# Own latents of the samples over all 128 rows, and new start addresses for the tiles that TensorE reads

## Chip, cores, metric

One NeuronCore of a Trainium2 chip runs the whole program in one launch. The metric is device time in microseconds (us) of that core, as the median of several runs. The profile is one further execution with the hardware profiler on. Engines are named as in the profile: PE (TensorE matmuls), PEld (TensorE weight loads), DVE (VectorE), ACT (ScalarE), POOL (GpSimd), SP (the queue that issues nearly all transfers).

## The reference, cut to what matters

Two layers (`DEPTH = 2`) of a streaming encoder for 256 prompt frames and 8 samples of 16 frames, 384 rows in all, width 1024:

```python
x += 0.5 * post_norm(SwiGLU(pre_norm(x)))      # FFN 1, D_FF = 2816
n  = pre_norm(x); h = n @ w_in                 # MLA, conv, gMLP, short conv, 4 gates
y  = sum_b sigmoid(gate_b) * (branch_b @ w_br_b);  x += post_norm(y @ w_o)
x += 0.5 * post_norm(SwiGLU(pre_norm(x)))      # FFN 2
# MLA of a sample: its 16 frames read 256 cached latents and their own 16
prob = softmax(mla_scores(q_nope, q_rope, concat([cache_lat, latent]), ...))
```

For a sample the kernel keeps everything in the latent space: the probabilities of its 128 rows (8 heads by 16 frames) over 256 cached and 16 own latents are multiplied by those 272 latents of 256 numbers.

## The kernel before

**Matmuls.** Each fp32 weight block is loaded into a staging tile `st` (4 buffers), rounded by ACT into `wh`, and DVE writes the rest, `st - wh`, as `wl`. Activations are split the same way (`xh`, `xl`; `hh`, `hl`; `mh`, `ml`; `bh*`, `bl*`). `mm3` (line 304) issues three fp32r matmuls for each product: high by high, low by high, high by low. `wh` and `wl` live in two rings: ring M (36 KB for each partition, mixer) and ring F (50 KB, feed-forward).

**Order.** The program hands every engine its instructions in an order written out by hand: a small planner (`tick`, `spawn`, `need`) counts estimated times and lets the follow-up work of ACT, DVE and POOL fall between PE's matmuls. PE's own order is a fixed stream with fillers.

**Stages of one layer.** `ffn_head` and `ffn_body` (line 489): for each of 20 chunks of hidden channels after the first two, two gate-up halves of 8 x 3 matmuls that stream 384 columns of `xh` or `xl` past a weight block (called "p" below), and 18 that stream 512 columns of a down weight past `hh` or `hl` ("d"). Heads (line 367) keep `xh` as the stationary operand and stream the weights. `mixer_front` (line 636) has the projections, the prompt's attention and the samples' attention, with `dense()` as the source of fillers; `mixer_merge` the gates (8 x 3 matmuls of 384 columns against a block of ring M) and the branch products; `mixer_out` the product with `w_o` (`mh`, `ml` stationary, 512 columns of ring M streaming).

**A sample's attention** (lines 1099 to 1137). `load_ct` loads the sample's cached latents `ct` and copies its 16 own rows of `lat_s` to partitions 0 to 15 of `nl` with a DMA. `sample` does the softmax over 272 columns. `sample_out` transposes the probabilities in three pieces, 128, 128 and 16 columns, copies them out (ACT two pieces into `ps[:, 0:2]`, DVE the 16 rows into `ps[0:S, 2]`), and multiplies: for each half k of the latents two fp32 matmuls over 128 rows (`ct`) and one over 16 rows (`nl`). In the trace each fp32 matmul stands as two.

**Addresses.** A tile occupies the same range in every partition, and pools stand one behind the other from byte 16512, each tile rounded up to 32 bytes. Adding up the sizes in the order of allocation gives where tiles start; a slice of 128 or 512 columns moves the start by a multiple of 512 bytes, so the place within 512 bytes is that of the tile:

| tiles | start, bytes past a multiple of 512, before | the same after, from the numbers in the diff |
|---|---|---|
| `xh`, `xl`, `ident`, `ones` | 192 | 0 |
| staging `st` | 448 | 192 |
| ring M `wh`, `wl` | 448 (8 `wl` at 192) | 0 (those 8 at 256) |
| `half` | 448 | 0 |
| ring F `wh`, `wl`; `hh`, `hl`; `bh*`, `bl*`; `aT`, `yT*` | 256 | 0 |
| `mh`, `ml` | 480 | 0 |
| `cqh`, `cql`, `lth`, `ltl`, `kT`, `qTp`, `qa` | 160 | a multiple of 64 |
| `qTs`, `lat_s`, `ct`, `pTs` | 32 | a multiple of 64 |

Of the kernel before, what the change touches and what calls it, by code (L numbers as in the profile page):

```python
# [8 lines left out]
F32 = mybir.dt.float32  # L9
F32R = mybir.dt.float32r  # L10
BF16 = mybir.dt.bfloat16
AF = mybir.ActivationFunctionType
ALU = mybir.AluOpType
AX = mybir.AxisListType
PSUM = bass.MemoryType.PSUM

P = 128
D = 1024
KD = D // P
T = 384  # L20
NT = 3
# [5 lines left out]
S = 16  # L27
NP = TP // S
PAST = 256
H = 8  # L30
ND = 64
RD = 32
QL = 384
KL = 256
CW = 31
SM_SCALE = (ND + RD) ** -0.5
NEG = -1e30
TAIL = 4
LAG = 2
RING_M = 36  # L40
RING_F = 50
STAGE = 4
# [4 lines left out]
PE, ACT, DVE, POOL = "tensor", "scalar", "vector", "gpsimd"  # L47
# [50 lines left out]
class Core:  # L98
    def __init__(self, tc, a, depth):
        self.tc, self.a, self.depth = tc, a, depth  # L100
        self.nc = Chip(self)


    def plan_units(self):

# [216 lines left out]
        return self.nt.tile([P, 512], F32, tag="half", name="half", bufs=4)  # L322

    def junk(self, n):
        return self.nt.tile([P, 512], BF16, tag="junk", name="junk", bufs=2)[:, :n]

    def bank(self):
        self.bk = (self.bk + 1) % 6
# [257 lines left out]
    def mixer_consts(self, l):  # L586
        nc, a = self.nc, self.a
        q = self.mc
        m = {}
        for name, shape in (("rows", [1152]), ("cols", [74]), ("gbias", [2, P]), ("wst", [4, P])):  # L590
            m[name] = q.tile([P] + shape, F32, tag=name, name=name)
        nc.sync.dma_start(out=m["rows"], in_=a["rows"][l].partition_broadcast(P))
        nc.sync.dma_start(out=m["cols"], in_=a["cols"][l])
        nc.sync.dma_start(out=m["gbias"], in_=a["gbias"][l])
        nc.sync.dma_start(out=m["wst"], in_=a["wst"][l])
        bd = m["bd"] = q.tile([P, 4, P], F32, tag="bd", name="bd")
        nc.gpsimd.memset(bd, 0.0)
        for b in range(NB):
            nc.sync.dma_start(out=bd[b * S:(b + 1) * S, :, b * S:(b + 1) * S], in_=a["wst"][l, 0:S, :, 0:S])
        nc.gpsimd.memset(m["wst"][64:128, :, 0:64], 0.0)  # L600
        return m
# [15 lines left out]
    def mixer(self, l, m):  # L617

        nc, tc, a = self.nc, self.tc, self.a
        pool = lambda name, bufs=1: tc.tile_pool(name=name, bufs=bufs, reuse_waits="tile")  # L620
        self.mo_ctx = tc.tile_pool(name="mixo", bufs=1, side="right", reuse_waits="tile")
        with pool("mixp") as mp:
            aT = mp.tile([P, 4, T], F32, name="aT")
            self.th = {(0, g): mp.tile([P, T], F32, name=f"th{g}") for g in range(3)}
            yT = {b: mp.tile([P, 2, T], F32, name="yT" + b) for b in "bcd"}
            with pool("mixf") as mf, pool("mixa") as ma:
                self.mixer_front(l, m, mf, ma, aT, yT)
            mo = self.mo_ctx.__enter__()
            mh = mo.tile([P, KD, T], F32R, name="mh")
            ml = mo.tile([P, KD, T], F32R, name="ml")  # L630
            with pool("mixm") as mm_:
                self.mixer_merge(l, mm_, aT, yT, mh, ml)
        self.open_ring()
        return self.mixer_out(l, mh, ml, self.load_gain(a["mix_norm_post"][l]))

    def mixer_front(self, l, m, mf, ma, aT, yT):
        nc, tc, a = self.nc, self.tc, self.a
        mm = nc.tensor.matmul
        rows, cols = m["rows"], m["cols"]
# [2 lines left out]
                                 cols[:, 66:68], cols[:, 68:74].rearrange("p (m k) -> p m k", m=2))  # L642
        pool = lambda name, bufs=1: tc.tile_pool(name=name, bufs=bufs, reuse_waits="tile")
        vn = [mf.tile([P, 256], F32, name=f"vn{t}") for t in range(NT)]
        qTs = ma.tile([P, 4, P], F32, name="qTs")
        qr0 = ma.tile([96, NB, H * S], F32, name="qr0")
        qrs = ma.tile([P, 2, H * S], F32, name="qrs")
        krT = ma.tile([96, T], F32, name="krT")
        lat_s = ma.tile([P, KL], F32, name="lat_s")
# [187 lines left out]
        with pool("mixq") as mq:  # L837
# [122 lines left out]
            for hp in range(4):  # L960
                w = self.weights(("uq", l, hp))
                for i in range(2):
                    h = 2 * hp + i
                    o = self.bank()[:, :T]
# [22 lines left out]
            for j in range(4):  # L987
                o = self.bank()[:, :TP]
# [5 lines left out]
            for t in range(2):  # L994
                o = self.bank()
# [78 lines left out]
        with pool("mixs") as ms:  # L1074
# [22 lines left out]
            cts = {}  # L1097

            def load_ct(b):
                ct = ms.tile([P, 2, KL], F32, tag="ct", name="ct", bufs=4)  # L1100
                nc.sync.dma_start(out=ct, in_=a["cache"][l, b].rearrange("(k p) c -> p k c", p=P))
                nl = ms.tile([S, KL], F32, tag="nl", name="nl", bufs=4)
                nc.sync.dma_start(out=nl, in_=lat_s[b * S:(b + 1) * S, :])
                cts[b] = ct, nl

            for b in range(2, 5):
                load_cT(b, ms)

            def sample(b, sb):
                ct, nl = cts.pop(b)  # L1110
                yield PE
                p = self.half()[:, :PAST + S].unsqueeze(1)
                yield from self.softmax(p, sb.unsqueeze(1), 1)
                self.drop("acc")
                self.spawn(("att",), sample_out(b, p, ct, nl))

            def sample_out(b, p, ct, nl):
                yield DVE
                pt = self.acc(2, 0)
                for k in range(2):  # L1120
                    nc.tensor.transpose(pt[:, k * P:(k + 1) * P], p[:, 0, k * P:(k + 1) * P], self.ident)
                nc.tensor.transpose(pt[0:S, 256:384], p[:, 0, PAST:], self.ident)
                self.drop("half")
                yield PE
                ps = ms.tile([P, 3, P], F32, tag="pTs", name="pTs", bufs=2)
                nc.scalar.copy(ps[:, 0:2, :], pt[:, 0:256].rearrange("p (a b) -> p a b", a=2))
                nc.vector.tensor_copy(ps[0:S, 2, :], pt[0:S, 256:384])
                self.drop("acc")
                yield ACT
                o = self.acc(2, 1)[:, :256].rearrange("p (a b) -> p a b", a=2)  # L1130
                for k in range(2):
                    ksl = slice(k * P, (k + 1) * P)
                    for kc in range(2):
                        mm(o[:, k, :], lhsT=ct[:, kc, ksl], rhs=ps[:, kc, :], start=(kc == 0), stop=False)
                    mm(o[:, k, :], lhsT=nl[:, ksl], rhs=ps[0:S, 2, :], start=False, stop=True)
                yield PE
                nc.scalar.copy(qa[:, :, b, :], o)

# [128 lines left out]
    def run(self):  # L1267
        nc, tc, a = self.nc, self.tc, self.a
        self.units = self.plan_units()
        self.index = {u[0]: i for i, u in enumerate(self.units)}  # L1270
        self.next_unit = self.at = 0
        self.staged, self.live, self.arrival = [], {}, 0.0
        self.spans, self.ring_at, self.size = {"M": {}, "F": {}}, {"M": 0, "F": 0}, {"M": RING_M * 1024, "F": RING_F * 1024}
        self.now, self.seq, self.busy, self.queue, self.idle = 0.0, 0, False, [], []
# [4 lines left out]
        with ExitStack() as es:  # L1279
            pool = lambda name, bufs=1, **kw: es.enter_context(tc.tile_pool(name=name, bufs=bufs, **kw))  # L1280
            const = pool("const")
            self.stage = pool("stage", STAGE)
            self.rings = {"M": pool("ringm").ring(RING_M * 1024), "F": None}
            self.nt = pool("nt")
            self.gains = pool("gains", 2)
# [4 lines left out]
            self.dummy = const.tile([P, 1], F32, name="dummy")  # L1290
            self.neghalf = const.tile([P, 1], F32, name="neghalf")
            nc.vector.memset(self.neghalf, -0.5)
            self.ones = const.tile([P, P], F32, name="ones")
            nc.vector.memset(self.ones, 1.0 / 256)
            self.x = [const.tile([P, D], F32, name=f"x{t}") for t in range(NT)]
# [5 lines left out]
            self.load_unit()  # L1301
            self.ident = const.tile([P, P], F32, name="ident")
            nc.scalar.dma_start(out=self.ident, in_=a["ident"])
            self.xh = const.tile([P, KD, T], F32R, name="xh")
            self.xl = const.tile([P, KD, T], F32R, name="xl")

# [18 lines left out]
            for l in range(self.depth):  # L1325
                m = {}

                def consts():
                    if l == 0:
                        self.rope_t = const.tile([P, NT, 2 * RD], F32, name="rope_t")  # L1330
                        nc.sync.dma_start(out=self.rope_t, in_=a["rope_t"])
                        self.rope_f = const.tile([P, T], F32, name="rope_f")
                        nc.sync.dma_start(out=self.rope_f, in_=a["rope_f"])
                    m.update(self.mixer_consts(l))

                self.ffn_head("ffn1", l)
                tail, post = self.ffn_body("ffn1", l, hook=consts)
                nc.scalar.activation(self.dummy, self.neghalf, AF.Exp)
                self.tails(tail, post, self.load_gain(a["mix_norm_pre"][l]))
                self.close_ffn_pool()  # L1340
                self.close_ring()
                tail, post = self.mixer(l, m)
                self.tails(tail, post, self.load_gain(a["ffn2_norm_pre"][l]))
                self.mo_ctx.__exit__(None, None, None)
                self.ffn_pool()
                self.ffn_head("ffn2", l)
                last = l + 1 == self.depth
                tail, post = self.ffn_body("ffn2", l, a["o_y"] if last else None)
                self.tails(tail, post, None if last else self.load_gain(a["ffn1_norm_pre"][l + 1]))
# [135 lines left out]
```

## Time and profile before

| | |
|---|---|
| three runs | 1886.31, 1886.86, 1892.37 us; median 1886.86 |
| the profiled execution | 1885.2 us, its span in the trace 1883.4 us |
| PE busy | 1858.1 us, 99% of the span |
| DVE, ACT, POOL busy | 964.1, 693.3, 73.8 us |
| granted TensorE clock, mean | 0.999 |

Busy times of PE overlap from one matmul to the next, since matmuls are pipelined: the mean of one (340 ns for 384 columns) is longer than the distance between two starts. What a matmul costs in a stream is the distance from its start to the next one's, read from a timeline.

### The profile page before, as it was taken

Reading aid. Unit: us, or ns where it says so; the run is one execution under the profiler, and the core shown is the slowest. Engines: PE = TensorE matmul, PEld = TensorE weight load, DVE = VectorE, ACT = ScalarE, POOL = GpSimd, SP = SyncE. Lnnn points to the kernel's source line nnn. Section 1 sums busy time; section 2 is a strip of 40 time slices with the busy share of each in tenths; the row PEclk is TensorE's granted clock in tenths of the full one; section 3 lists DMA queues with packets and bytes.
Section 4 is the critical chain, followed back from the end, with each engine's and each line's share of the span. In section 5 each row is a group of like instructions: output and inputs, shape, how many; then the busy total and the mean of one; then the engine's idle time right before and its main releaser. Section 6 shows DMA issues by size and latency. Waiting matters only on the chain.

```text
span 1883.4 us, 25172 instructions
## 1 busy us (share of the span) xinstructions
PE 1858.1 (99%) x10066; PEld 1723.3 (91%) x10066; DVE 964.1 (51%) x1472; ACT 693.3 (37%) x1146; POOL 73.8 (4%) x118
## 2 busy tenths in 40 slices
PE   8999999999999999999999999999999999999998
PEld 6999998978999889999989999988889998999997
DVE  5333347986554463333463333478864445533333
ACT  5333334443333443333343333434343335433332
POOL 0000001300000000000000000013000000000000
PEclk9999999999999999999999999999999999999999
DMA  7434443562334444344443444444514344433441
GB/s 255 132 124 129 128 145 86 149 174 78 107 125 136 145 149 130 126 123 123 134 135 124 133 124 124 126 100 134 174 60 137 121 139 134 146 123 124 128 128 45
DMA packets 99031, 243.12 MB, mean 129 GB/s; under 512 B 29281, under 2 KB 40673, under 8 KB 98914
## 3 DMA queue, kind: packets, MB, share of 16 engines
q1 hardware_dynamic: 98770, 241.45, 41.3%
q8 instruction: 79, 1.29, 0.3%
q14 instruction: 38, 0.31, 0.1%
q10 hardware_dynamic: 144, 0.07, 0.0%
HBM read 237.62 MB, written 3.31 MB: 128 GB/s over the span
## 4 chain that ended last, share of the span: by engine, by line
PE 92%; DVE 6%; ACT 1%; issue 1%; POOL 0%; DMA 0%; POOLq 0%; DVEq 0%; ACTq 0%
PE rot L72 59%; PE acc L72 33%; DVE yTb L72 1%; DVE wl L72 1%; DVE half L72 1%; DVE sx L72 0%; ACT half L72 0%; DVE sv L72 0%; DVE qTp L72 0%; DVE xl L72 0%; DVE yTd L72 0%; DVE qa L72 0%; DVE kT L72 0%; POOL kv L72 0%; ACT qTs L72 0%
## 5 line engine op out<-in xcount | busy, mean ns | idle before, releaser
L72 DVE TENSOR_TENSOR wl<-st,wh 128x1024 fp32r<-128x1024 f32 (+3 forms) x428 | 502.2, 1184 | 481.8 <-ACT wh L72 479.0
L72 ACT CAST wh<-st 128x1024 fp32r<-128x1024 f32 (+3 forms) x428 | 430.6, 1017 | 679.3 <-issue 372.0
L72 PE MATMUL rot<-xh,wh 128*128 128x384 f32 x1984 | 674.7, 340 | 0.8 <-ACT sg L72 0.7
L72 PE MATMUL rot<-xh,wl 128*128 128x384 f32 x1984 | 670.4, 338 | 0.0
L72 PE MATMUL rot<-xl,wh 128*128 128x384 f32 x1984 | 669.9, 338 | 0.0
L72 PEld LDWEIGHTS rot<-xh,wh 128*128 128x128 f32 x1984 | 372.0, 188 | 8.9 <-issue 3.5
L72 PEld LDWEIGHTS rot<-xh,wl 128*128 128x128 f32 x1984 | 372.3, 188 | 4.1 <-issue 0.5
L72 PEld LDWEIGHTS rot<-xl,wh 128*128 128x128 f32 x1984 | 372.1, 188 | 1.1 <-issue 0.5
L72 PE MATMUL acc<-wh,hl 128*128 128x512 f32 x528 | 205.8, 390 | 0.0
L72 PE MATMUL acc<-wl,hh 128*128 128x512 f32 x528 | 205.7, 390 | 0.0
L72 PE MATMUL acc<-wh,hh 128*128 128x512 f32 x528 | 205.5, 389 | 0.0
L72 DVE TENSOR_TENSOR hf<-sg,rot 128x384 f32<-128x384 f32 x80 | 44.4, 555 | 152.5 <-PE rot L72 152.5
L72 PEld LDWEIGHTS acc<-wl,hh 128*128 128x128 f32 x528 | 99.1, 188 | 20.4
L72 PEld LDWEIGHTS acc<-wh,hh 128*128 128x128 f32 x528 | 99.1, 188 | 17.7
L72 PEld LDWEIGHTS acc<-wh,hl 128*128 128x128 f32 x528 | 99.1, 188 | 17.6
L72 ACT ACTIVATE half<-rot 128x384 f32<-128x384 f32 x58 | 28.6, 493 | 167.1 <-PE rot L72 167.1
L72 DVE SCALAR_TENSOR_TENSOR half<-half,acc 128x384 f32<-128x384 f32 x44 | 24.4, 554 | 126.2 <-PE acc L72 126.2
L72 DVE SCALAR_TENSOR_TENSOR yTb<-bs,cols,yTb 128x384 f32<-128x384 f32 x120 | 74.8, 623 | 2.2
L72 POOL TENSOR_TENSOR post<-post,neghalf 128x1 f32<-128x1 f32 x18 | 11.6, 645 | 1455.9 <-DVE post L72 1455.9
L72 PE MATMUL rot<-wl,xh 128*128 128x512 f32 (+1 forms) x144 | 55.8, 388 | 1.5 <-DVE wl L72 1.5
L72 PE MATMUL rot<-wh,xh 128*128 128x512 f32 (+1 forms) x144 | 56.2, 390 | 0.0
L72 PE MATMUL acc<-ident,half 128*128 128x128 f32 (+1 forms) x266 | 43.4, 283 | 7.2 <-DVE half L72 7.2
(211 smaller groups left out, 1665.3 us busy)
## 6 DMA issues: line engine op xcount, KB each, us to landing
st<-ffn_gp SPq DMA_DIRECT2D x160, 512.0 KB, 3.5
st<-ffn_dn SPq DMA_DIRECT2D x88, 512.0 KB, 3.5
st<-in_g SPq DMA_DIRECT2D x64, 512.0 KB, 3.7
st<-in_f SPq DMA_DIRECT2D x24, 512.0 KB, 4.4
st<-ffn_gs SPq DMA_DIRECT2D x16, 512.0 KB, 5.1
st<-w_o SPq DMA_DIRECT2D x16, 512.0 KB, 4.8
st<-w_br SPq DMA_DIRECT2D x16, 384.0 KB, 3.1
st<-in_b SPq DMA_DIRECT2D x8, 512.0 KB, 4.5
```

The costliest lines, as they stand in the source:

```text
L72: r = f(*args, **kw)
```

## The change

**Samples.** `nl` and its 16 DMAs go. A tile `pn` with four slots of 128 columns is zeroed once in each layer; the sample's 16 own probabilities are scaled into columns `b*16` to `b*16+15` of slot `b % 4`, so that the third piece is a full 128 x 128 transpose and the third matmul runs over all 128 rows of `lat_s`. The scaling becomes two instructions (256 and 16 columns); a slot's old columns are zeroed again by POOL from sample 4 on; the copy out of PSUM is one ACT instruction of 384 columns, and DVE's copy goes.

**Addresses.** `align` inserts tiles that nothing uses. `rope_t` and `rope_f` are allocated earlier (their loads stay where they were), `cols` grows from 74 to 128 columns, and `junk` has one buffer where it had two.

```diff
+GRID = 512
+TOP = 229344
...
+    def align(self, pool, at, grid, off=0):
+
+        n = at % grid if at == TOP else (off - at) % grid
+        if n:
+            self.pads += 1
+            pool.tile([P, n // 4], F32, name=f"pad{self.pads}")
...
-        return self.nt.tile([P, 512], BF16, tag="junk", name="junk", bufs=2)[:, :n]
+        return self.nt.tile([P, 512], BF16, tag="junk", name="junk", bufs=1)[:, :n]
...
-        for name, shape in (("rows", [1152]), ("cols", [74]), ("gbias", [2, P]), ("wst", [4, P])):
+        for name, shape in (("rows", [1152]), ("cols", [128]), ("gbias", [2, P]), ("wst", [4, P])):
...
             ml = mo.tile([P, KD, T], F32R, name="ml")
+            self.align(mo, TOP, GRID)
...
+        self.align(ma, 416, GRID)
         qTs = ma.tile([P, 4, P], F32, name="qTs")
...
-                nl = ms.tile([S, KL], F32, tag="nl", name="nl", bufs=4)
-                nc.sync.dma_start(out=nl, in_=lat_s[b * S:(b + 1) * S, :])
-                cts[b] = ct, nl
+                cts[b] = ct
...
+            pn = ms.tile([P, 4, P], F32, name="pn")
+            nc.gpsimd.memset(pn, 0.0)
+
             def sample(b, sb):
-                ct, nl = cts.pop(b)
-                yield PE
-                p = self.half()[:, :PAST + S].unsqueeze(1)
-                yield from self.softmax(p, sb.unsqueeze(1), 1)
+                ct = cts.pop(b)
+                yield PE
+                p = self.half()[:, :PAST + S]
+                sx = self.small.tile([P, 3], F32, tag="sx", name="sx")
+                mx, sm, rc = (sx[:, i:i + 1] for i in range(3))
+                own = pn[:, b % 4, :]
+                if b >= 4:
+                    nc.gpsimd.memset(own[:, (b - 4) * S:(b - 3) * S], 0.0)
+                nc.vector.tensor_reduce(mx, sb, axis=AX.X, op=ALU.max, negate=True)
+                yield DVE
+                nc.scalar.activation(p, sb, AF.Exp, bias=mx, accum_out=sm)
+                yield ACT
+                nc.vector.reciprocal(rc, sm)
+                nc.vector.tensor_scalar(p[:, :PAST], p[:, :PAST], rc, None, op0=ALU.mult)
+                nc.vector.tensor_scalar(own[:, b * S:(b + 1) * S], p[:, PAST:], rc, None, op0=ALU.mult)
                 self.drop("acc")
...
-                for k in range(2):
-                    nc.tensor.transpose(pt[:, k * P:(k + 1) * P], p[:, 0, k * P:(k + 1) * P], self.ident)
-                nc.tensor.transpose(pt[0:S, 256:384], p[:, 0, PAST:], self.ident)
+                for k in range(3):
+                    nc.tensor.transpose(pt[:, k * P:(k + 1) * P], p[:, k * P:(k + 1) * P] if k < 2 else own, self.ident)
...
-                nc.scalar.copy(ps[:, 0:2, :], pt[:, 0:256].rearrange("p (a b) -> p a b", a=2))
-                nc.vector.tensor_copy(ps[0:S, 2, :], pt[0:S, 256:384])
+                nc.scalar.copy(ps, pt.rearrange("p (a b) -> p a b", a=3))
...
-                    for kc in range(2):
-                        mm(o[:, k, :], lhsT=ct[:, kc, ksl], rhs=ps[:, kc, :], start=(kc == 0), stop=False)
-                    mm(o[:, k, :], lhsT=nl[:, ksl], rhs=ps[0:S, 2, :], start=False, stop=True)
+                    for kc in range(3):
+                        mm(o[:, k, :], lhsT=ct[:, kc, ksl] if kc < 2 else lat_s[:, ksl], rhs=ps[:, kc, :],
+                           start=(kc == 0), stop=(kc == 2))
...
+            self.align(pool("pad"), 57344, GRID, 192)
             self.stage = pool("stage", STAGE)
+            self.align(pool("pad2"), 57536 + STAGE * 4096, GRID)
...
+            self.align(const, 16576, GRID)
             self.ones = const.tile([P, P], F32, name="ones")
...
+            self.rope_t = const.tile([P, NT, 2 * RD], F32, name="rope_t")
+            self.rope_f = const.tile([P, T], F32, name="rope_f")
+            self.align(const, 32512, GRID)
             self.xh = const.tile([P, KD, T], F32R, name="xh")
```

## Rows read from the trace of the kernel before

**Rows 1.** The page: busy time by engine, granted clock, chain by engine.

```profile
PE 1858.1 (99%) x10066; PEld 1723.3 (91%) x10066; DVE 964.1 (51%) x1472; ACT 693.3 (37%) x1146; POOL 73.8 (4%) x118
...
PEclk9999999999999999999999999999999999999999
...
PE 92%; DVE 6%; ACT 1%; issue 1%; POOL 0%; DMA 0%; POOLq 0%; DVEq 0%; ACTq 0%
```

**Rows 2.** PE's waits: what for, us in total, times, longest.

```profile
PE acc L72 <- DVE half L72: 7.2, 10, 2.3
...
PE acc L72 <- DVE pTs L72: 1.0, 2, 0.5
```

**Rows 3.** PE groups by shape: busy us, mean ns; idle before.

```profile
L72 PE MATMUL rot<-xh,wh 128*128 128x384 f32 x1984 | 674.7, 340 | 0.8 <-ACT sg L72 0.7
...
L72 PE MATMUL acc<-wh,hl 128*128 128x512 f32 x528 | 205.8, 390 | 0.0
...
L72 PE MATMUL acc<-wh,mh 128*128 128x512 f32 x96 | 38.0, 395 | 0.0
...
L72 PE MATMUL acc<-pTs,ct 128*128 128x128 f32 x128 | 21.3, 289 | 0.0
...
L72 PE MATMUL acc<-pTs,nl 16*128 16x128 f32 x64 | 15.5, 321 | 1.0 <-DVE pTs L72 1.0
```

**Rows 4.** PE timeline, feed-forward: 18 "d" matmuls, then 48 "p" (start us, us).

```profile
141.86 0.39 PE L72 MATMUL acc<-wh,hh 128*128 128x512 f32 x1
...
145.94 0.34 PE L72 MATMUL rot<-xh,wh 128*128 128x384 f32 x1
...
154.42 0.39 PE L72 MATMUL acc<-wh,hh 128*128 128x512 f32 x1
```

**Rows 5.** PE timeline, merge: 12 of a branch, 24 of a gate, 6 branch.

```profile
542.43 0.33 PE L72 MATMUL acc<-bha,wh 128*128 128x384 f32 x1
...
544.50 0.34 PE L72 MATMUL rot<-xh,wh 128*128 128x384 f32 x1
...
548.69 0.33 PE L72 MATMUL acc<-bhd,wh 128*128 128x384 f32 x1
...
549.72 0.34 PE L72 MATMUL rot<-xh,wh 128*128 128x384 f32 x1
```

**Rows 6.** PE timeline, product with w_o: first and 25th of a run.

```profile
1566.99 0.40 PE L72 MATMUL acc<-wh,mh 128*128 128x512 f32 x1
...
1572.59 0.40 PE L72 MATMUL acc<-wh,mh 128*128 128x512 f32 x1
```

**Rows 7.** PE timeline, head of a feed-forward: first and 17th of a run.

```profile
673.18 0.39 PE L72 MATMUL rot<-wh,xh 128*128 128x512 f32 x1
...
676.84 0.86 PE L72 MATMUL rot<-wh,xl 128*128 128x512 f32 x3
```

**Rows 8.** PE timeline, one sample's product with its latents.

```profile
1370.92 0.60 PE L72 MATMUL acc<-pTs,ct 128*128 128x128 f32 x4
1371.45 0.48 PE L72 MATMUL acc<-pTs,nl 16*128 16x128 f32 x2
1371.87 0.71 PE L72 MATMUL acc<-pTs,ct 128*128 128x128 f32 x4
1372.51 0.48 PE L72 MATMUL acc<-pTs,nl 16*128 16x128 f32 x2
1372.92 0.55 PE L72 MATMUL acc<-ident,half 128*128 128x128 f32 x3
```

**Rows 9.** Groups by shape of POOL, ACT and DVE: busy us, mean ns.

```profile
L72 POOL MEMSET bd<- 128x512 f32 x2 | 1.1, 535 | 0.0
...
L72 POOL MEMSET bs<- 128x28 f32 x2 | 0.3, 132 | 0.0
...
L72 ACT COPY pTs<-acc 128x256 f32<-128x256 f32 x16 | 6.0, 373 | 13.9 <-PE acc L72 13.7
...
L72 ACT COPY cg<-rot 128x384 f32<-128x384 f32 x4 | 1.9, 482 | 0.3 <-PE rot L72 0.3
...
L72 DVE COPY pTs<-acc 16x128 f32<-16x128 f32 x16 | 4.4, 276 | 14.5 <-ACT pTs L72 14.5
...
L72 DVE RECIPROCAL sx<-sx 128x1 f32<-128x1 f32 x16 | 2.4, 153 | 0.4 <-ACT half L72 0.4
```

More of the change, by code (lines that the diff above doesn't have):

```diff
@@ L589, in mixer_consts @@
         m = {}
-        for name, shape in (("rows", [1152]), ("cols", [74]), ("gbias", [2, P]), ("wst", [4, P])):
+        for name, shape in (("rows", [1152]), ("cols", [128]), ("gbias", [2, P]), ("wst", [4, P])):
             m[name] = q.tile([P] + shape, F32, tag=name, name=name)
         nc.sync.dma_start(out=m["rows"], in_=a["rows"][l].partition_broadcast(P))
-        nc.sync.dma_start(out=m["cols"], in_=a["cols"][l])
+        nc.sync.dma_start(out=m["cols"][:, :74], in_=a["cols"][l])
         nc.sync.dma_start(out=m["gbias"], in_=a["gbias"][l])
@@ L1101, in load_ct, with sample_out @@
                 nc.sync.dma_start(out=ct, in_=a["cache"][l, b].rearrange("(k p) c -> p k c", p=P))
-                nl = ms.tile([S, KL], F32, tag="nl", name="nl", bufs=4)
-                nc.sync.dma_start(out=nl, in_=lat_s[b * S:(b + 1) * S, :])
-                cts[b] = ct, nl
+                cts[b] = ct
             for b in range(2, 5):
                 load_cT(b, ms)
+            pn = ms.tile([P, 4, P], F32, name="pn")
+            nc.gpsimd.memset(pn, 0.0)
             def sample(b, sb):
-                ct, nl = cts.pop(b)
+                ct = cts.pop(b)
                 yield PE
-                p = self.half()[:, :PAST + S].unsqueeze(1)
-                yield from self.softmax(p, sb.unsqueeze(1), 1)
+                p = self.half()[:, :PAST + S]
[11 more added lines that the diff above has]
+                nc.vector.tensor_scalar(own[:, b * S:(b + 1) * S], p[:, PAST:], rc, None, op0=ALU.mult)
                 self.drop("acc")
-                self.spawn(("att",), sample_out(b, p, ct, nl))
-            def sample_out(b, p, ct, nl):
+                self.spawn(("att",), sample_out(b, p, own, ct))
+            def sample_out(b, p, own, ct):
                 yield DVE
-                pt = self.acc(2, 0)
-                for k in range(2):
-                    nc.tensor.transpose(pt[:, k * P:(k + 1) * P], p[:, 0, k * P:(k + 1) * P], self.ident)
-                nc.tensor.transpose(pt[0:S, 256:384], p[:, 0, PAST:], self.ident)
+                pt = self.acc(2, 0)[:, :3 * P]
+                for k in range(3):
+                    nc.tensor.transpose(pt[:, k * P:(k + 1) * P], p[:, k * P:(k + 1) * P] if k < 2 else own, self.ident)
                 self.drop("half")
@@ L1270, in run @@
         self.index = {u[0]: i for i, u in enumerate(self.units)}
-        self.next_unit = self.at = 0
+        self.next_unit = self.at = self.pads = 0
         self.staged, self.live, self.arrival = [], {}, 0.0
@@ L1329, in consts @@
                     if l == 0:
-                        self.rope_t = const.tile([P, NT, 2 * RD], F32, name="rope_t")
                         nc.sync.dma_start(out=self.rope_t, in_=a["rope_t"])
-                        self.rope_f = const.tile([P, T], F32, name="rope_f")
                         nc.sync.dma_start(out=self.rope_f, in_=a["rope_f"])
```

## The prediction

> **What bounds the kernel now.** I read the page first. PE is busy for 1858.1 of 1883.4 us, the chain that ended last lies on PE for 92%, and the granted clock is full (2.4 GHz) in all slices [rows 1]. The reader is to see that only what shortens PE's stream counts: DVE is half busy and POOL nearly idle. Then PE's waits: the longest entry is 7.2 us in ten waits, the entry that this change touches 1.0 us [rows 2]. So there is hardly a wait to remove; what is left is the price of a matmul in the stream. The groups by shape give the counts [rows 3], but their mean durations overlap, so I took prices from the timeline, as distances between starts.
>
> Those distances are not all alike for the same work:
>
> - "d", 512 columns, stationary `hh` and streaming weights both 256 bytes past a multiple of 512: (145.94 - 141.86) / 18 = 226.7 ns [rows 4].
> - "p", 384 columns, streaming `xh` at 192, weights at 256: (154.42 - 145.94) / 48 = 176.7 ns [rows 4].
> - Gates, 384 columns, the same `xh` at 192, weights of ring M at 448: (548.69 - 544.50) / 24 = 174.6 ns; branches, streaming at 256, weights at 448: (544.50 - 542.43) / 12 = 172.5 and (549.72 - 548.69) / 6 = 171.7 ns [rows 5].
> - w_o, 512 columns, stationary `mh` at 480, streaming at 448: 5.60 / 24 = 233.3 ns [rows 6].
> - Heads, 512 columns, stationary `xh` at 192, streaming at 256: 3.66 / 16 = 228.8 ns [rows 7].
>
> "p" and the gates have the same shape, the same moving tile and the same PSUM buffers; ACT and DVE split weights beside both. "d" and w_o differ only in their tiles. What differs is the place of the two operands, so I take the place as the cause. That is a reading of five stretches, not a measurement of one change.
>
> **The change part by part: addresses.** Afterwards nearly all fp32r operands start at 0 modulo 512: stationary and streaming tile stand at the same place. The only stretch that has this relation now is "d" (256 and 256), and it is the cheapest of the 512-column stretches. For 384 columns no row has it. Bounds: the worst is that equal places do to 384 columns what 480 against 448 does to w_o, 6.6 ns over the cheapest; the best is that the whole overhead goes. The columns alone cost (226.7 - 172.1) / 128 = 0.43 ns each by the cheapest rows, so 384 would be 164 ns, 12.7 ns under "p". Between these I take the middle of gates and branches, 173.3 ns, because "d" shows that equal places bring a 512-column stream to its cheapest, and these are the cheapest of 384.
>
> - "p": 20 chunks x 2 halves x 24 matmuls x 4 feed-forwards = 3,840, each 176.7 - 173.3 = 3.4 ns: 13.1 us.
> - Gates and projections: 5,952 (3 x 1,984 in [rows 3]) - 3,840 = 2,112, each 174.6 - 173.3 = 1.3 ns: 2.7 us. Branches, 480, each 172.1 to 173.3: 0.6 us lost.
> - w_o: 3 x 96 = 288 [rows 3], each 233.3 - 226.7 = 6.6 ns: 1.9 us.
> - Heads of the feed-forwards: 288, each 2.1 ns: 0.6 us.
> - "d", 3 x 528 = 1,584 [rows 3]: nothing, they are at 226.7 already.
>
> Together 17.7 us. All of it is on PE's path, and no transfer has to come sooner than it can: the feed-forward's stream gets 1 to 2% faster while ACT and DVE are half idle [rows 1].
>
> The staging tiles move from 448 to 192. From ring F they stood 192 bytes away before and do so after; from ring M it was 0. That concerns ACT and DVE, which have room: nothing. `cols`, the earlier allocation of `rope_t` and `rope_f` and the unused tiles issue no instruction. `junk` with one buffer is written by ACT alone, in order: nothing; if ACT had to wait, it would be for its own last write.
>
> Here a page of the Trainium skill speaks against the whole part: "SBUF — State Buffer", section "SBUF: two separate sides", and "TensorE: Matmul & The Clock Gate", "Step-by-step", hold that TensorE loads weights and streams through two read ports of its own, and that nothing but DVE and GpSimd's shared port contends. By that, a tile's place costs nothing and this sum would be 0 in place of 17.7 us; the 4 ns between "p" and the branches [rows 4, 5] don't agree with it, unless something other than the place makes them.
>
> **The samples' product.** In the row of one sample each half k should be six equal fp32 matmuls. Four over `ct` run from 1370.92 to 1371.45; with the two over 16 rows and what follows them, the first half lasts 1371.87 - 1370.92 = 0.95 us and the second 1372.51 - 1371.87 + 0.41 = 1.05 us [rows 8]. The cheap ones stand 0.11 us apart (0.60 us for four, of which 0.27 is the length of the last), so six take 0.67 us in a uniform stream. The 16-row form costs 0.28 and 0.38 us more in the two halves, and the stretch behind, to the transposes, is slowed a little too, since the second block of four also lasts 0.71 in place of 0.60 us (that is inside the 0.38). Saved: 0.66 us for a sample, 16 samples: 10.6 us. The contraction over 128 rows has the same shape as `ct`'s, which fixes its price; the full third transpose lies 0.11 us from the next like the 16-column one, so it adds nothing.
>
> Around it, off PE: ACT copies 384 columns in one piece, 482 in place of 373 ns [rows 9], 0.11 us later for PE; but the piece that PE waited for was DVE's (1.0 us in two waits [rows 2]), and that goes. I cost it at nothing, because fillers of the dense part run meanwhile; uncovered it would be 16 x 0.11 = 1.7 us. DVE loses 16 copies of 276 ns and gains 16 small scalings, between 153 ns (one column) and 276 ns (128 columns): at most even. POOL zeroes `pn` twice at 0.54 us and a slot's 16 columns eight times at no more than 0.13 us [rows 9]; the copies of latents into `cT` queue behind it, and POOL is 4% busy. The zeroing comes a softmax ahead of DVE's scaling. On SP 16 small DMAs go, each of which stood in the queue between a load of `ct` and the next load of weights; PE hardly waits for weights, so nothing.
>
> **Sum.** The profiled execution took 1885.2 us. 1885.2 - 17.7 - 10.6 = 1856.9; the median of the runs stands 1.7 us above the profiled one, so 1858.6 us. I forecast **1858.5 us**.
>
> **Rivals.**
>
> - *The place is not the cause* (or the new places miss): "p" stays at 176.7 ns, only the samples gain: 1886.9 - 10.6 = 1876 us. For it: the page above, and that no row has 384 columns with equal places. Against it: the stretches in [rows 4 to 7] fall apart by tile and not by stage.
> - *Equal places collide.* Ends on the other side. If an LDWEIGHTS and the stream beside it start at the same place and hinder each other by x ns above the cheapest, all some 9,100 fp32r matmuls pay x, against a gain of 28.3 us: it turns at x = 3.1 ns. At the 6.6 ns of w_o [rows 6] it is 60 us, so 1886.9 - 28.3 + 60 = 1919 us. Against it: "d" has equal places and is cheap [rows 4].
> - *The samples gain nothing*, because PE then waits for the longer chain POOL, DVE, ACT: addresses alone, 1869 us. Against it: PE has fillers there.
> - *More than the difference of today's rows*: a start at 0 removes part of the overhead that all rows have. At half of the bound for 384 columns, some 5 ns further on the 9,100, it is 45 us more: 1813 us. For it: no stretch has 0 now. Against it: five different pairs of places all stop at 172 to 177 and 227 to 233 ns.
>
> **How the numbers follow.** Forecast 0.60, for which I take 1848 to 1870 us (half to one and a half of the 17.7, the samples between 8 and 12). Place not the cause 0.15, samples gain nothing 0.08, more than that 0.08, collision 0.07, and 0.02 for anything else. The range 1846 to 1878 holds the forecast, the first and the third rival, 0.83. Within 0.3% (5.7 us, about what a measurement of this kernel can tell from no change) lies a partial collision or half a gain of the samples alone: 0.05. Slower 0.07, faster 0.88.
>
> **What the next profile would show.** Right: a run of 48 "p" in 8.3 us (173 ns each) where it was 8.48, w_o at 227 ns, the samples' blocks of twelve fp32 matmuls in 1.3 to 1.4 us, PE still at 99%. "p" at 176.7 would refute the address part, "d" above 227 would be the collision, idle PE ahead of `pTs` the longer chain. Wrong I would be above all if equal places behave otherwise at 0 than at 256, or if the 384-column stream differs from the 512-column one in where it meets the weight load.

## The result, and the profile after

The changed kernel takes **1861.8 us** (median of four runs, 1861.56 to 1863.88; the profiled execution is the slowest of them) against 1886.6 us beside it (1885.15 to 1892.37). The ratio is 0.9865, 95% interval 0.9844 to 0.9887: 24.8 us less. The forecast was 1858.5 us, its range 1846 to 1878.

The page of the changed kernel, with the lines that answer to [rows 1]:

```profile
PE 1835.8 (99%) x10066; PEld 1707.8 (92%) x10066; DVE 961.5 (52%) x1472; ACT 695.8 (37%) x1146; POOL 76.9 (4%) x128
...
PEclk9999999999999999999999999999999999999999
...
PE 92%; DVE 5%; ACT 1%; issue 1%; POOL 0%; DMA 0%; POOLq 0%; DVEq 0%; ACTq 0%
```

PE has as many instructions as before, is 99% busy still, and is 22.3 us shorter. Its waits (for what, us in all, times, longest) show what stands where the wait of [rows 2] for DVE's copy stood:

```profile
PE acc L74 <- DVE half L74: 7.7, 9, 2.3
...
PE acc L74 <- DVE pn L74: 1.0, 2, 0.5
```

The last transpose waits for DVE's scaling into `pn` as long as the product waited for DVE's copy, 1.0 us. The nine entries together come to 19.2 us where they were 18.0, so waits gave nothing; the price of matmuls changed. Groups of PE by shape (busy us, mean ns), to be held against [rows 3]:

```profile
L74 PE MATMUL rot<-xh,wh 128*128 128x384 f32 x1984 | 669.1, 337 | 0.7 <-ACT sg L74 0.7
...
L74 PE MATMUL acc<-wl,hh 128*128 128x512 f32 x528 | 207.2, 393 | 0.0
L74 PE MATMUL acc<-wh,hl 128*128 128x512 f32 x528 | 207.1, 392 | 0.0
...
L74 PE MATMUL acc<-pTs,ct 128*128 128x128 f32 x128 | 19.7, 276 | 0.0
...
L74 PE MATMUL acc<-pTs,lat_s 128*128 128x128 f32 x64 | 12.4, 275 | 0.0
```

384 columns got cheaper, the samples' product too, and "d", costed at nothing, got dearer. Distances between starts say by how much. The timeline of one chunk (18 "d", 48 "p", next "d"), beside [rows 4]:

```profile
141.23 0.39 PE L74 MATMUL acc<-wh,hh 128*128 128x512 f32 x1
...
143.31 0.39 PE L74 MATMUL acc<-wh,hh 128*128 128x512 f32 x1
...
145.35 0.33 PE L74 MATMUL rot<-xh,wh 128*128 128x384 f32 x1
...
146.42 0.33 PE L74 MATMUL rot<-xh,wh 128*128 128x384 f32 x1
...
153.70 0.39 PE L74 MATMUL acc<-wh,hh 128*128 128x512 f32 x1
```

"p" takes (153.70 - 145.35) / 48 = 174.0 ns where it was 176.7. But it isn't even: the first six take 1.07 / 6 = 178 ns, the other 42 take 7.28 / 42 = 173.3. "d" likewise: the first nine 2.08 / 9 = 231 ns, the last nine 2.04 / 9 = 226.7. Matmul by matmul, the medians over 72 such chunks are 229, 233, 236, 224, 231, 236, 228, 232, 231 and then 227 ns for "d", and 171, 175, 177, 185, 176, 182 and then 173 ns for "p". I call this the irregular start. The kernel before has none of it here: 226.8 and 176.7 ns from one end to the other.

One sample's product in the changed kernel, for [rows 8]:

```profile
1360.32 0.61 PE L74 MATMUL acc<-pTs,ct 128*128 128x128 f32 x4
1360.76 0.39 PE L74 MATMUL acc<-pTs,lat_s 128*128 128x128 f32 x2
1360.98 0.61 PE L74 MATMUL acc<-pTs,ct 128*128 128x128 f32 x4
1361.43 0.39 PE L74 MATMUL acc<-pTs,lat_s 128*128 128x128 f32 x2
1361.65 0.38 PE L74 MATMUL acc<-ident,half 128*128 128x128 f32 x2
1361.87 0.27 PE L74 MATMUL acc<-ident,pn 128*128 128x128 f32 x1
```

Twelve fp32 matmuls take 1361.65 - 1360.32 = 1.33 us, 111 ns each, where they took 2.00 us.

Adding the distances between starts over the whole trace, by the kind of matmul that begins each, gives where the time came from:

| kind | forecast, us | measured, us |
|---|---|---|
| samples' product, 192 | -10.6 | 33.41 to 20.78: -12.6, of which 1.1 are the two waits for DVE's copy that stood inside it |
| "p", 3,832 in such stretches | -13.1 | 676.9 to 666.6: -10.3 |
| gates and projections, 2,120 | -2.7 | 385.1 to 384.0: -1.1; -1.6 in the run `st_0` below, whose clock did not fall among them as it did here for 3.4 us |
| "d", 1,584 | 0 | +3.0 |
| w_o, 288 | -1.9 | -0.3; -1.4 in `st_0`, without a wait of 1.1 us that fell into this one |
| branches; heads with all that is left | 0.0 | +0.3; -0.2 |
| first to last start | -28.3 | 1873.6 to 1852.3: -21.2; -23.5 in `st_0` |

### The profile page after: what moved, and what is told of

It is laid out like the page before. It is cut to its first block, busy times and chain, and to the rows that moved or that the text cites. A ratio compares the mean times of both kernels' runs of the same rounds, so it can differ in the third digit from the quotient of the medians.

```text
span 1862.1 us, 25158 instructions
## 1 busy us (share of the span) xinstructions
PE 1835.8 (99%) x10066; PEld 1707.8 (92%) x10066; DVE 961.5 (52%) x1472; ACT 695.8 (37%) x1146; POOL 76.9 (4%) x128
## 4 chain that ended last, share of the span: by engine, by line
PE 92%; DVE 5%; ACT 1%; issue 1%; POOL 0%; DMA 0%; POOLq 0%; DVEq 0%; ACTq 0%
PE rot L74 59%; PE acc L74 33%; DVE wl L74 1%; DVE yTb L74 1%; DVE half L74 1%; DMA st<-ffn_gs 0%; ACT wh L74 0%; ACT junk L74 0%; DVE sv L74 0%; DVE sx L74 0%; DVE qTp L74 0%; DVE yTd L74 0%; DVE qa L74 0%; DVE xl L74 0%; POOL kv L74 0%
## 5 line engine op out<-in xcount | busy, mean ns | idle before, releaser
L74 PEld LDWEIGHTS acc<-wh,hl 128*128 128x128 f32 x528 | 99.1, 188 | 19.2
L74 PE MATMUL acc<-ident,half 128*128 128x128 f32 x250 | 41.5, 282 | 8.6 <-DVE half L74 7.7
## 6 DMA issues: line engine op xcount, KB each, us to landing
st<-w_br SPq DMA_DIRECT2D x16, 384.0 KB, 3.1
```

The source lines that it names most:

```text
L74: r = f(*args, **kw)
```

## The experiments

Places are given as **distance**: the start of the streaming tile less that of the stationary one. Each kernel was timed in several rounds beside the kernel before.

**1. Each half of the change alone.** `samples_only` is the changed kernel with every tile where it was before; `addresses_only` has the samples as they were before.

```diff
 samples_only (against the changed kernel)
-        if n:
+        if n and False:
...
-        ... tag="junk", name="junk", bufs=1)
+        ... tag="junk", name="junk", bufs=2)
-        ... ("cols", [128]), ...
+        ... ("cols", [74]), ...
...
 addresses_only (against the changed kernel): nl, softmax, sample_out of the kernel before
```

> Only the samples' part of the change, all tiles where they were before. Theory (the 16-row product drains PE's pipeline around itself, and the place of operands is a separate gain): PE's time in the fp32 products of the samples falls by 12 to 13 us as it did in the full change (33.4 to 20.8 us summed over start distances), the span by 10 to 13 us, about 1874 us; runs of 48 p matmuls stay at 8.48 us and w_o at 233 ns. Rival (PE then waits for the longer chain POOL, DVE, ACT): the products get as short, but the span falls by less than 6 us. Rival (the gain of the full change came from addresses of the samples' tiles): the products stay near 33 us.

> Only the new places, with the 16-row product and its DMAs as before. Theory: the rest of the full change's gain, 10 to 13 us, about 1874 us; p in 8.35 us for 48, w_o at 227 ns, d at 229 ns instead of 227. Rival (place has no effect of its own): 1886 us and p at 8.48 us. If the two parts add up, the sum of both gains is that of the full change, 24 to 25 us, within 3 us.

Samples alone: 1872.0 us (1871.86 to 1872.19), ratio 0.9913 (0.9898 to 0.9929). In the trace the samples' product falls by 12.65 us, the whole by 13.2, and "p" stays at 176.67 ns. Addresses alone: 1880.7 us (1875.65 to 1881.99, six runs), ratio 0.9955 (0.994 to 0.997). There "p" is 173.87 ns (mean over the 48) and "d" 228.94, the pattern of the changed kernel to the ns, and w_o -1.3 us. The spread of its runs comes from stretches at half clock (last section); by the lowest runs the parts are worth 1885.1 - 1871.9 = 13.2 and 1885.1 - 1875.65 = 9.5 us, together 22.7 of the 23.5 us that both give. They add.

**2. One pair of tiles moved, forward and back.** `x_448` is the changed kernel with `xh` and `xl` back at a distance of -64 from the weights; `before_x_256` is the kernel before with only these two moved onto the weights' place.

```diff
 x_448 (against the changed kernel)
-            self.align(const, 32512, GRID)
+            self.align(const, 32512, GRID, 448)
             self.xh = ...
             self.xl = ...
+            self.align(const, 57280, GRID)
 before_x_256 (against the kernel before)
+            const.tile([P, 16], F32, name="pad1")
             self.xh = ...
             self.xl = ...
+            const.tile([P, 112], F32, name="pad2")
             (and junk with bufs=1)
```

> The changed kernel with xh and xl alone 64 bytes lower (448 in place of 0 past a multiple of 512; all else stays). p then has the distance between streaming and stationary tile that it had before (64 bytes lower). Theory A (the distance of the two places within 512 bytes sets the price): p goes back to 8.48 us for 48 (176.7 ns), gates of ring M go from 173.4 to about 176.7 ns too, d goes back to 226.8 ns because the irregular first matmuls behind p vanish; together 11 + 7 - 3.4 = some 14 us slower than the changed kernel, 1876 us. Theory B (a start at 0 of 512 is what counts for each operand by itself): p and gates worse by an amount that the trace of before doesn't tell, d stays at 229 ns. Theory C (place of xh is of no account, another moved tile made the gain): 1862 us.

> The kernel before with xh and xl alone 64 bytes higher (256 in place of 192 past a multiple of 512, where ring F stands; one buffer of junk less makes room). Equal places, but none at 0. Theory A (distance counts): p falls from 176.7 to about 173.9 ns with irregular first matmuls, d rises from 226.8 to 229 ns, gates (256 against 448) stay within 172 to 174 ns: 10.7 - 3.4 + 1 = some 8 us faster than before, 1878 us. Theory B (a start at 0 counts): no gain, p stays at 176.7 ns or above.

`x_448`: 1870.1 us (1869.46 to 1871.36), ratio 0.9902 (0.9884 to 0.992). The timeline of one of its chunks:

```profile
54.09 0.39 PE L74 MATMUL acc<-wh,hh 128*128 128x512 f32 x1
...
58.17 0.34 PE L74 MATMUL rot<-xh,wh 128*128 128x384 f32 x1
...
66.65 0.39 PE L74 MATMUL acc<-wh,hh 128*128 128x512 f32 x1
```

4.08 us for 18 and 8.48 us for 48: 226.7 and 176.7 ns, the numbers of [rows 4], with no irregular start. But the time is 6 us below the 1876 us of theory A, and the part that failed is the gates. They stand at -64 like "p", with the same shape and streaming tile, and were to cost 176.7 ns too; of the 7 us expected for them and the projections hardly anything came (0.3 us against the trace of `st_0`). One gate of this run, its first matmul and the branch behind it:

```profile
538.02 0.33 PE L74 MATMUL rot<-xh,wh 128*128 128x384 f32 x1
...
542.17 0.34 PE L74 MATMUL acc<-bhd,wh 128*128 128x384 f32 x1
```

4.15 / 24 = 172.9 ns, and 173.2 ns is the mean of 56 such gates. Most projections cost 173 to 175 ns here, but two runs of 84 of them, over weights of the same ring, cost 176.7. So the distance alone does not fix the price: at -64 it is 173 or 176.7 ns, and no run shows what tells the two apart.

`before_x_256` shows the reverse, the changed kernel's pattern in the kernel before:

```profile
54.09 0.39 PE L72 MATMUL acc<-wh,hh 128*128 128x512 f32 x1
...
58.22 0.33 PE L72 MATMUL rot<-xh,wh 128*128 128x384 f32 x1
...
66.56 0.39 PE L72 MATMUL acc<-wh,hh 128*128 128x512 f32 x1
```

It takes 1878.3 us (1877.6 to 1883.85), ratio 0.9952 (0.9935 to 0.9968): by the lowest runs 7.5 of the 9.5 us of all addresses. So for "p" the place is the cause, and moving `xh` and `xl` gives most of the gain. "d" is touched by neither edit, and yet goes from 226.8 to 228.9 ns when "p" comes to equal places: what precedes a stretch counts too.

**3. Which property of the place.** All are the changed kernel with one pair of tiles, or the staging tiles, elsewhere: `x_256` (xh and xl at 256, weights at 0), `x_320`, `x_384`, `st_0` (staging at 0, where it was 192 beside), `mh_480` (mh and ml at 480, as before).

```diff
 x_256, x_320, x_384: o = 256, 320, 384
-            self.align(const, 32512, GRID)
+            self.align(const, 32512, GRID, o)
             (and a tile behind xl that keeps what follows where it was)
 st_0
-            self.align(pool("pad"), 57344, GRID, 192)
+            self.align(pool("pad"), 57344, GRID, 0)
...
 mh_480
-            self.align(mo, TOP, GRID)
```

> The changed kernel with xh and xl alone at 256 past a multiple of 512 (the distance that the gates had before: 174 ns with some irregular first matmuls; heads from ring M at 227 to 228). Theory A: p about 174 ns, heads and mB about 227 ns; d depends on whether the irregular start vanishes: 226.8 (then 1859 us) or 229 (then 1862 us). Rival (equal places only): p 176 ns or more, 1870 us.

> The changed kernel with xh and xl alone at 320 past a multiple of 512 (192 lower than the weights' place, the distance that the branches had before: 172 to 173.7 ns). Theory A (the distance of the places decides, and one distance has one price for 384 columns): p about 173.3 ns in its steady part; if the irregular first matmuls of p and d belong to distance 0, they vanish, d is 226.8 and p 173.3 throughout, 5 to 6 us gained, and heads and the mB projection (stationary xh, distance 192 the other way, 233 ns in the run with xh moved in the kernel before) lose up to 432 x 5 ns = 2 us: about 1858 us. Rival (equal places are the only cheap ones): p 176 ns or more, 1870 us.

> The changed kernel with xh and xl at 384 past a multiple of 512: 128 bytes, half of the period of 256 that the runs so far suggest, from the weights in either direction. Theory D (only the distance of the streaming tile behind the stationary one counts, and a stream that begins below the stationary tile pays): +128 and -128 are the same place, so p lies at 173.3 ns as with +64 or at 176.7 ns as with -64; the first predicts 1860 us and no irregular start of a stretch, the second 1870 us. Theory D2 (the price grows with the distance): p between 173.4 and 176.7 ns, heads above 229 ns, 1862 to 1870 us. Rival: a start at a multiple of 128 is a place of its own, whatever the distance, and p and d look as in the changed kernel (irregular start, d 228.9 ns, 1862 us).

> The changed kernel with the staging tiles at 0 in place of 192 bytes past a multiple of 512; every tile that TensorE reads stays where it is modulo 512. Theory (TensorE doesn't read staging tiles; ACT and DVE have room): p, d and w_o unchanged to 1 ns, casts and subtractions 1.05 and 1.22 us as before, 1861 to 1863 us. Rival (reads of the staging tiles by ACT and DVE meet TensorE's reads): p or d dearer by 1 to 3 ns, 1866 us or more.

> The changed kernel with mh and ml left at 480 past a multiple of 512, as in the kernel before, while the weights of w_o stream from 0: a distance of +32 bytes where it was -32 before and is 0 after. Theory D (the distance counts): w_o between 227 and 229 ns, the time within 0.6 us of the changed kernel's. Rival (the start of mh, no multiple of 64, made the 233.3 ns): w_o at 233 ns again, 288 x 6 ns = 1.7 us more than the changed kernel. Everything else as in the changed kernel.

`x_256`: 1862.1 us (1861.43 to 1863.2), ratio 0.9862 (0.9842 to 0.9881), "d" 228.94 and "p" 173.87 ns: equal to distance 0 matmul by matmul. The pattern repeats at 256 bytes; what the diff calls a grid of 512 needs only half of that.

`x_320`, a distance of +64 modulo 256, is the fastest of all: **1860.0 us** (1859.69 to 1860.45), ratio 0.985 (0.9831 to 0.987).

```profile
54.02 0.39 PE L74 MATMUL acc<-wh,hh 128*128 128x512 f32 x1
...
58.11 0.34 PE L74 MATMUL rot<-xh,wh 128*128 128x384 f32 x1
...
66.43 0.39 PE L74 MATMUL acc<-wh,hh 128*128 128x512 f32 x1
```

"p" takes 8.32 / 48 = 173.3 ns and "d" 4.09 / 18 = 227.2: the irregular start is nearly gone. It pays elsewhere: branches (+1.1 us against the changed kernel), which get an irregular start behind the gates, and heads (+1.0), whose 512 columns now stream at -64. The projection with stationary `xh` has the same shape and distance:

```profile
318.78 0.39 PE L74 MATMUL acc<-wh,xh 128*128 128x512 f32 x1
...
324.37 0.40 PE L74 MATMUL acc<-wh,xh 128*128 128x512 f32 x1
```

5.59 / 24 = 233 ns, and the heads are at 233 too.

`x_384`, half of the period away: 1872.1 us (1871.79 to 1872.66), ratio 0.9923 (0.9907 to 0.994).

```profile
54.37 0.40 PE L74 MATMUL acc<-wh,hh 128*128 128x512 f32 x1
...
58.46 0.34 PE L74 MATMUL rot<-xh,wh 128*128 128x384 f32 x1
...
66.89 0.40 PE L74 MATMUL acc<-wh,hh 128*128 128x512 f32 x1
```

8.43 / 48 = 175.6 ns, in a steady round of 174, 175 and 178. The projection with stationary `xh`, 512 columns:

```profile
321.05 0.39 PE L74 MATMUL acc<-wh,xh 128*128 128x512 f32 x1
...
326.62 0.39 PE L74 MATMUL acc<-wh,xh 128*128 128x512 f32 x1
```

5.57 / 24 = 232 ns, and the heads are at 232 to 233. Both prices lie where theory D2 had them, but its rule, that the price grows with the distance, does not hold: 128 costs less than -64 (175.6 against 176.7 ns for "p"). The rival that a start at a multiple of 128 is as good as equal places is out. The time came 2 us above D2's bound: gates cost 176.0 ns where they cost 173.3, which with the projections is 4.0 us against the changed kernel, and heads lost as well.

`st_0`: 1861.8 us (1861.45 to 1862.74), ratio 0.986 (0.9841 to 0.988). Rounding and splitting of the weights, by shape:

```profile
L74 ACT CAST wh<-st 128x1024 fp32r<-128x1024 f32 x380 | 397.2, 1050 | 671.5 <-issue 369.5 <-PE rot L74 262.1 <-PE acc L74 33.8
...
L74 DVE TENSOR_TENSOR wl<-st,wh 128x1024 fp32r<-128x1024 f32 x380 | 463.9, 1224 | 473.9 <-ACT wh L74 472.1 <-issue 0.7
```

In the changed kernel they take 1048 and 1223 ns. The 192 bytes beside change nothing.

`mh_480`: 1863.3 us (1862.77 to 1863.49), ratio 0.9877 (0.9862 to 0.9891). Its product with w_o, the first and the 25th of a run:

```profile
1543.49 0.40 PE L74 MATMUL acc<-wh,mh 128*128 128x512 f32 x1
...
1549.09 0.39 PE L74 MATMUL acc<-wh,mh 128*128 128x512 f32 x1
```

5.60 / 24 = 233.3 ns, that of [rows 6], though the distance went from -32 to +32; the changed kernel has (1567.53 - 1562.09) / 24 = 226.7. My expectation by distance alone, 227 to 229, fell. Whether a distance of 32 costs this in either direction, or the start of `mh` at no multiple of 64, no run here tells apart.

What a matmul in a stream costs, all runs together (ns, distance modulo 256):

| distance | 384 columns | 512 columns |
|---|---|---|
| 0 | 173.3 after an irregular start | 226.8 after an irregular start |
| +64 | 173.3 ("p", `x_320`) | 229 (heads, before and `x_448`) |
| -64 | 176.7 ("p", before and `x_448`); 173.2 (gates, `x_448`) | 233 (heads, `x_320`) |
| 128 | 175.5 ("p", `x_384`); 176.0 (gates, `x_384`) | 232 to 233 (heads, `x_384`) |
| +32, -32 | not run | 233.3 (w_o, `mh_480` and before) |

**4. What is dear about 16 rows.** `nl_adjacent` is the kernel before with the two 16-row products next to each other: two changes between 128 and 16 rows for a sample in place of four, the same matmuls.

```diff
-                    for kc in range(2):
-                        mm(o[:, k, :], lhsT=ct[:, kc, ksl], rhs=ps[:, kc, :], start=(kc == 0), stop=False)
-                    mm(o[:, k, :], lhsT=nl[:, ksl], rhs=ps[0:S, 2, :], start=False, stop=True)
+                    for kc in ((0, 1, 2), (2, 0, 1))[k]:
+                        lt, r = (ct[:, kc, ksl], ps[:, kc, :]) if kc < 2 else (nl[:, ksl], ps[0:S, 2, :])
+                        mm(o[:, k, :], lhsT=lt, rhs=r, start=(kc == 2 * k), stop=(kc == 2 - k))
```

> The kernel before with one change: in a sample's product the two 16-row matmuls stand side by side (first half: ct, ct, nl; second half: nl, ct, ct), so the array changes between 128 and 16 rows twice per sample in place of four times. Theory S (each change of row count drains the stream, on top of what the 16-row form itself costs): the 12 instructions of a sample go from 2.00 us to about 1.80 us (some 0.19 us of one change back and forth saved), 16 x 0.19 = 3 us off the span, 1882 to 1884 us. Rival F (each 16-row matmul costs twice as much, wherever it stands; no price for the change): 2.00 us as before, span as before.

1880.9 us (1880.24 to 1884.11, eight runs), ratio 0.9965 (0.9953 to 0.9978). One sample:

```profile
1378.70 0.60 PE L72 MATMUL acc<-pTs,ct 128*128 128x128 f32 x4
1379.24 0.71 PE L72 MATMUL acc<-pTs,nl 16*128 16x128 f32 x4
1379.87 0.71 PE L72 MATMUL acc<-pTs,ct 128*128 128x128 f32 x4
1380.42 0.81 PE L72 MATMUL rot<-dg,ones 128*128 128x384 f32 x2
```

Four 16-row matmuls take 0.63 us where two took 0.42 [rows 8]. One by one, the distances from the last matmul over `ct` on are 205, 213, 112, 112, 200, 213 and 112 ns: inside a run of its own kind a 16-row matmul costs 112 ns, as one over 128 rows. So rival F is out. A change to 16 rows costs (205 - 112) + (213 - 112) = 194 ns, over two matmuls, and the change back (200 - 112) + (213 - 112) = 189. The Trainium skill, "TensorEngine Tiling (Array Packing)", "Key Properties", holds that changing the tiling mode drains TensorE, without a price; the trace agrees, if a change of the row count is such a change, with 194 and 189 ns.

Four changes would be 0.77 us for a sample and 12.3 us for 16, an estimate from these distances. The 12.6 us measured come close to it partly by chance: 1.1 us of them are waits for DVE's copy (two distances of 782 and 761 ns where the others are 205), and the second half of the fourth change lies behind the product, where the next transpose takes 165 ns in place of 109. Within the twelve matmuls three and a half changes make 2.00 us out of 1.34. Here the sum of the samples' products falls from 33.41 to 28.59 us (the twelve of the sample above take 1.72 us), 4.8 us less; the expectation said 3, from two changes taken at 0.19 us together, where each of them costs that much.

## Why the prediction was right, step by step

**The bound** was right: PE's stream decides, one wait of 1.0 us took the place of another, nothing off PE mattered. ACT's longer copy (480 ns), POOL's zeroing (106 ns for a slot's columns, 525 for all of `pn`) and the missing DMAs left no mark on the end.

**The place as the cause** was a reading of five stretches; `x_448` and `before_x_256` show it by moving one pair of tiles. The rival that place costs nothing, 1876 us, is out. "SBUF — State Buffer" ("SBUF: two separate sides") and "TensorE: Matmul & The Clock Gate" ("Step-by-step") of the Trainium skill speak of two read ports of TensorE that don't contend; what the prediction drew from that, that a place costs nothing, does not hold here, since "p" pays 3.3 ns of 176.7 for it. Whether the ports are where it arises, no run shows. That equal places are the cheapest held for "p" only in part: +64 is as cheap, and `x_320` is the faster kernel.

**"p", 13.1 us: mis-sized, 10.3.** The steady price was 173.3 ns as taken, but the mean is 173.9, because the first six after "d" cost 26 ns more together (1,066 in place of 1,040). In 80 chunks that is 2.1 of the 2.8 us that were missing.

**"d", nothing: mis-sized, +3.0 us.** The price 226.7 ns stayed, and the irregular start came on top, nine matmuls with 39 ns together (2,080 in place of 2,041), 3.4 us if all 88 stretches had it. "d" had equal places before too, without that start; what is new is that the "p" ahead of it has them as well. The rival "equal places collide" had this much in it: a few matmuls get dearer at a change of stretch, and not all 9,100.

**Gates and projections, 2.7 us: mis-sized, 1.1** (1.6 in `st_0`), and the step that led there was wrong. It said that no row has 384 columns with equal places. The gates had: streaming at 192, weights at 448, modulo 256 the same place. The trace of the kernel before showed it, had I read the gates one by one and not as a mean over 24 (timeline, merge, between two rows of [rows 5]):

```profile
545.02 0.34 PE L72 MATMUL rot<-xh,wh 128*128 128x384 f32 x1
545.20 0.35 PE L72 MATMUL rot<-xh,wl 128*128 128x384 f32 x1
545.38 0.34 PE L72 MATMUL rot<-xl,wh 128*128 128x384 f32 x1
545.56 0.34 PE L72 MATMUL rot<-xh,wh 128*128 128x384 f32 x1
545.74 0.33 PE L72 MATMUL rot<-xh,wl 128*128 128x384 f32 x1
```

545.74 - 545.02 = 0.72 us for four, 180 ns each; behind them it is 173.3. That is the irregular start already, so 174.6 ns was 173.3 and a start, and only the start could be saved. In the changed kernel branch and gate stand at the same distance, and the gates run even:

```profile
536.99 0.33 PE L74 MATMUL rot<-xh,wh 128*128 128x384 f32 x1
...
541.15 0.33 PE L74 MATMUL acc<-bhd,wh 128*128 128x384 f32 x1
```

24 in 541.15 - 536.99 = 4.16 us, 173.3 ns each.

**Samples, 10.6 us: mis-sized, 12.6.** I held 2.00 us against a uniform 1.34 and took the rest as the price of the 16-row form. It is the price of the changes between forms, and the change back to the transposes lies behind the stretch that I measured. Of the 2.0 us more, 1.1 are the waits for DVE's copy, which the prediction saw go and costed at nothing; 1.0 us of waits stands ahead of the last transpose instead.

**w_o, 1.9 us**, came to 1.4: the steady 226.7 ns behind the same irregular start. **Branches and heads** were too small to matter.

The errors partly cancelled: 2.0 us too little for the samples, 7.4 too much for "p", "d", gates and w_o (the last two from `st_0`). The trace of `st_0`, free of the stray wait, is 4.8 us short of the 28.3; in the medians 3.5 us are missing (24.8 of 28.3), because the median of the kernel before stands 1.4 us above its lowest run and that of the changed kernel 0.2. Open is what makes the irregular start. It was seen at distance 0 behind another shape ("d" and "p") or another distance (branch and gate, before), and its length hangs on the stretch ahead: for "d" it costs 39 ns behind "p" at 0, 11 behind "p" at +64 (`x_320`), none behind "p" at -64. At +64 the first six of "p" are uneven too, but cost nothing together (1,041 ns). Open as well is why a place costs anything, and why -64 costs "p" 3.3 ns and most gates nothing.

## What to carry to other kernels

In a stream of matmuls that each load weights, read prices as distances between starts, one by one at the head of a stretch and in its middle: a mean hides a start that belongs to the change of stretch. Move one pair of tiles at a time, modulo 256 bytes: here a streaming tile 64 bytes above the weights was as good as equal places, with a start that cost almost nothing, and 64 below cost "p" 3.3 ns for each matmul but the gates of the same run nothing. So a price found in one stretch has to be read again in the next. A matmul over few rows is not dear in itself; the changes to and from it are, so group them or fill the rows with zeros.

## What was not expected of the hardware

The granted clock falls by half inside the samples' stage in some executions. In `addresses_only` it does so for 13.7 us (busy us and instructions by engine, granted clock, DMA share, GB/s, for four stretches):

```profile
1340.00:1355.00 15.00, 15.00 (x90) 12.64 (x90) 10.25 (x24) 5.45 (x13) 0.65 (x1) 1.00 0.55 171
1355.00:1370.00 15.00, 15.00 (x88) 12.84 (x87) 11.29 (x24) 3.29 (x9) 0.00 (x0) 1.00 0.23 73
1373.70:1387.40 13.70, 13.70 (x47) 11.40 (x46) 6.12 (x17) 2.44 (x6) 1.33 (x1) 0.50 0.09 29
1387.40:1400.00 12.60, 12.60 (x93) 11.93 (x93) 6.18 (x11) 5.83 (x10) 0.00 (x0) 1.00 0.26 92
```

PE was busy for all of the 30 us of the first two stretches and for 3.3 of the 3.7 us behind them, at 2.4 GHz, and then ran at 1.2 GHz: 47 matmuls in 13.7 us, where 88 in 15 us would be 80. That is (80 - 47) x 15 / 88 = 5.6 us lost, an estimate from these rows. `before_x_256` has the same from 447.0 to 460.7 us. Kernels with the 16-row product vary accordingly (the kernel before 1885.0 to 1892.9 us over all rounds, `addresses_only` 1875.65 to 1881.99); with the full-row product no kernel's runs lie more than 2.4 us apart, and the one fall in the middle of the changed kernel's profiled execution lasts 3.4 us. The full-row product thus seems to have spared a fall besides its 12.6 us, which no run here shows alone.
